# RWKV state chain of a hybrid decoder block: full 128x128 products in place of 32-column and 64-row ones

## Chip, cores and metric

One core of a Trainium2 chip runs the whole block. The metric is the device time of one execution in microseconds; three executions were timed, and one more was recorded by the hardware profiler.

## The reference, cut to what matters

The block takes 512 tokens of width 1024. It projects them, runs two groups of heads side by side (a sparse attention, "NSA", and a recurrent time mix, "RWKV-7"), joins both in an output projection, and ends with a gated feed-forward layer. The part that is changed is the recurrence, over 8 heads of 64:

```python
def _wkv7_step(state, inp):
    r, w, k, v, a, b = inp
    sa = jnp.einsum('bhvk,bhk->bhv', state, a)
    state = state * w[:, :, None, :] + sa[..., None] * b[:, :, None, :] + v[..., None] * k[:, :, None, :]
    return state, jnp.einsum('bhvk,bhk->bhv', state, r)
...
    _, y = lax.scan(_wkv7_step, state0, xs)
...
    mu = jnp.mean(y, axis=-1, keepdims=True)
    var = jnp.mean(jnp.square(y - mu), axis=-1, keepdims=True)
    y = ((y - mu) * lax.rsqrt(var + GN_EPS)).reshape(B, T, D_RWKV) * ln_w + ln_b
```

## The kernel before, in words

The recurrence is not run token by token. The 512 tokens are cut into 16 chunks of 32, and the 8 heads into four pairs `JJ[j]` of 128 rows; two pairs make a group `GG[g]` (g = 0, 1). `prep(j)` makes for each pair the decayed vectors: `AR` holds, by chunk c, 32 columns of a~ and 32 columns of r~ over the 128 rows of the two heads; `BKt` holds, by pair of chunks cp, 128 rows: for each of its two chunks 32 rows of b~ and 32 rows of k~; `UV` has the same rows, 32 of u (to be found) and 32 of v. `inverse(g)` solves the triangular system inside each chunk (a loop of 31 steps on DVE and POOL with a way through DRAM), and leaves `AR` with the solved a~ and `AV` with the part of u that does not depend on the state.

`chain(g)` then walks over the 16 chunks. `step(c)` does: product `pu` (tiles named rw<-Sb,AR: the 32 columns of a~ against the state `Sb`, for both pairs), a DVE addition of `AV` into `UV` (the u of this chunk), product `pd` (rw<-UV,BKt: the chunk's 64 rows of b~ and k~ against its 64 rows of u and v), and two DVE additions of `pd` to the decayed state `sw`, which give the next `Sb`. So `pu`, `UV`, `pd`, `Sb` follow each other 15 times, and all else has to fit around them. `y(py, cp)` makes the output of two chunks: products py<-UV,Mr (64 columns each) and, for each chunk, py<-Sb,AR (32 columns of r~ against the state), all summed in one PSUM tile `py`. `norm` normalizes four chunks (128 tokens), transposes them and multiplies by the gate.

A product's shape is written rows*columns of its stationary operand. In the whole program most are 128*128; `pu` and py<-Sb,AR are 128*32, `pd` is 64*128, py<-UV,Mr, rw<-UV,Ma and rw<-XT,At are 128*64. A product of f32 operands shows as two records in the trace, of f32r operands as one.

The order of the work is not that of the code. Every call on an engine is held by `_Order` and released in the order of `TURNS`, a packed list of numbers, and `SWAP` names those `tensor_tensor` calls that go to the other of DVE and POOL. So chain(0) runs beside the rest of `prep` and the input projection, and chain(1) beside the attention (`score`, `attend`: products mm<-K,Q, rp<-cct,L, ot<-ph,Vt, with ACT's casts `ph` and DVE's `pl` between). Every record carries line 210, the one that makes the held calls, so the profile is read by tile names.

Of the kernel before, what the change touches and what calls it, by code (L numbers as in the profile page):

```python
# [33 lines left out]
for _n, _w in (("ident", 128), ("mask", 128), ("reset", 512), ("sel", 2), ("ones", 1), ("row", 1)):  # L34
# [91 lines left out]
    "jDS=@xD7x)pvEUZZZEtKg}l2QgcWKerAzul2eLlq-5p2Y|;z8&>tgp2AQeT^)-G@(*`_->Jl?mC$kl!1Nk{n$CK{5!n~~m*m{3`OWSK>bkLVL1KVjm+EjC"
    "WSvzTC?a6XIc)z{Ap!Kz?XBMf!*%{6C@@pKxHf*(9ZAHw|**ZtR!ycsI^OBp4W+bgYTAhC!rscIXdDFaU9*5&e&rB>}zv`KOTGza2?&3aEY<@m@2#Js(oG"
    "XL%1>??Fut2)AZ=-P6{u^!0Ym{;>Ue%W7P3pTJ_1lA=J;M5bQU9v{rd%-^vNs*5nfsrSrmJ?<)TWDe;W@Q=RsW!j?W`fz;8{&T0;Y;0!U*UDOnT1^<TMc;"
    "7fm##*3y}r#C^NSIN-WRJg)t8B&CVLdGfT0H0N;Dli-;o6GV{G6lB>%Mjeg=Nl)MpZc=;sDQP}D@h2|u{<|E{e0V49C7(clj;>q5j7g#Y3=_lk<`|9vx}0"
    "lGgoqr2l_KUR#N(dalSF$3cjf<2IY~gI`GhNIDM^JTB%@gm$ERdDcHs*wB^y1TdA=bNFo%pL+sS0l2Od{C^y?ga;#r6+TnYAh;^^_0V>j06AI!yCz0Zb+F"  # L130
    "cDwrHMu6E@rAxZ+iqsYVx!K(LC&57*vXm`F%i=-gUrPu&heUNmyYGiF$FW!NjDt}^c${yj&azh6DZ|d7*A%Szbw$<a4k&11a)`%;!WvI`p}C`)q(KnBy~1"
    "20&j3Gb{4miy~S1REoqFtZdKzd)k6BnyLcCkShux(N$YVH`h!|rm3pIzG?9PmlXx4Wpb~}p@(1}fzqXYg$g7P|OUjTgD9wJqZc2)yF=s<@DK2S{2FWo39Z"
    "g45g;zBgBNihCq$s^-DTz&b4vq%&#U)XXJg*H*E>jd0NgaBdGN`CK&>Z7X-8gbEqIHx+Rb!J%Xf&$eSw^wt%$=kdjnT5^lkj-P=+pEkvr*U-^^`T)8P{fH"
    "be#s-k(@DON<Bm`Hzhn<GSK%vfka89)efPB=QM?p!{jgn=$oHnoVQX}(gQ>?-Yb9<dP7oZIzQj?Q1ch%qU6MH^r7)SuFj8NB!N+4GJdW|ieMaYkF8{5-Ft"
    "j`ZnQ=Yw%8JFa86!E6uKn+B<Cd#j<!hwW4aDWb$yiZt)BJ#2*)A$N)F2fALTk9{2km}UrtYX#e2a`y2o?aGgG$7*>F6X1BWU1tDLV-V7;u7b+TU8a+U9hw"
    "X&L5>tz-1&gN`bjWw7rOJx;paTzUgDpq;c>Jr-GaXrqbt<dEO?x`-;zR0NQ0yVQ)=VLxb$W6V)nD>25@^ft*J|t^2#0OZdAqGloX)7zV6+dU`NXFS`m<`O"
    "JRZn1@@g8TPbJa25^S#dd8=q+<sU+KVH`%M}?F{XN-RdmzH+9_53FN4@!8oqDM;N;t(H3Zd4xFinwWIbyJFSm@Fb>Nt6-=Cdst5Hy`nm4p(Td}=ljmu=g|"
# [1145 lines left out]
```

## Time and profile before

| what | value |
|---|---|
| three timed executions | 792.83, 798.37, 799.33 us, median 798.37 |
| profiled execution, its own time | 796.21 us |
| its span | 794.3 us |
| PE busy | 766.3 us, 96% of the span |
| DVE, ACT, POOL busy | 517.5, 359.6, 227.0 us |

The chains lie in the first 380 us: chain(0) from about 170 to 255, chain(1) from about 302 to 372. From there on the output projection and the feed-forward layer run, with PE busy nearly all the time. The span is the time between the first and the last record; the execution's own time is 1.9 us more.

### The profile page before, as it was taken

Reading aid. Unit: us, or ns where it says so; the run is one execution under the profiler, and the core shown is the slowest. Engines: PE = TensorE matmul, PEld = TensorE weight load, DVE = VectorE, ACT = ScalarE, POOL = GpSimd, SP = SyncE. Lnnn points to the kernel's source line nnn. Section 1 sums busy time; section 2 is a strip of 40 time slices with the busy share of each in tenths; the row PEclk is TensorE's granted clock in tenths of the full one; section 3 lists DMA queues with packets and bytes.
Section 4 is the critical chain, followed back from the end, with each engine's and each line's share of the span. In section 5 each row is a group of like instructions: output and inputs, shape, how many; then the busy total and the mean of one; then the engine's idle time right before and its main releaser. Section 6 shows DMA issues by size and latency. Waiting matters only on the chain.

```text
span 794.3 us, 12056 instructions
## 1 busy us (share of the span) xinstructions
PE 766.3 (96%) x4152; PEld 617.0 (78%) x4152; DVE 517.5 (65%) x1078; ACT 359.6 (45%) x779; POOL 227.0 (29%) x360
## 2 busy tenths in 40 slices
PE   8999999999799889999999999999999999999998
PEld 7878768887567678777788888888888888888886
DVE  5565786788878978887264876767766777143131
ACT  5435644465234766766452544444444445131120
POOL 3334353234767766786414000000000000000000
PEclk9999999999879999999999999999999999999999
DMA  6542214321123030002442223232222324153130
GB/s 211 168 157 88 83 51 85 82 59 34 26 49 57 14 67 2 14 15 94 145 133 80 94 92 104 82 106 90 97 87 99 105 83 126 46 172 129 44 119 27
DMA packets 59708, 67.87 MB, mean 85 GB/s; under 512 B 25710, under 2 KB 32686, under 8 KB 59648
## 3 DMA queue, kind: packets, MB, share of 16 engines
q1 hardware_dynamic: 59460, 67.10, 27.4%
q8 instruction: 33, 0.54, 0.3%
q14 instruction: 27, 0.22, 0.1%
q10 hardware_dynamic: 188, 0.02, 0.0%
HBM read 63.91 MB, written 3.18 MB: 84 GB/s over the span
## 4 chain that ended last, share of the span: by engine, by line
PE 86%; DVE 7%; POOL 3%; issue 2%; ACT 1%; DMA 1%; SPq 0%; DVEq 0%; POOLq 0%; ACTq 0%
PE mm L210 31%; PE rp L210 23%; PE rw L210 21%; PE ot L210 5%; PE pre L210 4%; PE py L210 2%; POOL Z L210 1%; DVE Z L210 1%; DVE sgw L210 1%; DMA raw<-in_wst 1%; DVE Sb L210 0%; DVE sw L210 0%; DVE Ma L210 0%; DVE UV L210 0%; DVE qd L210 0%
## 5 line engine op out<-in xcount | busy, mean ns | idle before, releaser
L210 ACT CAST hi<-raw 128x512 fp32r<-128x512 f32 (+3 forms) x212 | 117.4, 584 | 127.2 <-DMA raw<-in_fdn 67.2
L210 DVE TENSOR_TENSOR lo<-raw,hi 128x512 fp32r<-128x512 f32 (+3 forms) x179 | 118.3, 672 | 39.8 <-ACT hi L210 15.4
L210 DVE SCALAR_TENSOR_TENSOR uf<-zf,fvt,uf 128x512 f32<-128x512 f32 x88 | 65.7, 749 | 29.4 <-ACT uf L210 29.4
L210 ACT ACTIVATE uf<-zf,fvt 128x512 f32<-128x512 f32 x44 | 35.8, 816 | 98.4 <-DVE zf L210 98.4
L210 POOL MEMSET zf<- 128x2 f32 x44 | 4.2, 100 | 211.3 <-DVE uf L210 107.5
L210 POOL TENSOR_TENSOR lo<-raw,hi 128x512 fp32r<-128x512 f32 (+3 forms) x33 | 39.8, 1210 | 68.3 <-ACT hi L210 28.8
L210 PE MATMUL mm<-act,hi 128*128 128x512 f32 x176 | 55.2, 395 | 0.0
L210 PE MATMUL mm<-h2h,hi 128*128 128x512 f32 x128 | 50.7, 396 | 0.0
L210 PE MATMUL mm<-h2l,hi 128*128 128x512 f32 x128 | 50.5, 395 | 0.0
L210 PE MATMUL mm<-h2h,lo 128*128 128x512 f32 x128 | 50.5, 394 | 0.0
L210 PE MATMUL rw<-h2h,hi 128*128 128x512 f32 x112 | 44.3, 395 | 0.0
L210 PE MATMUL rp<-h2l,hi 128*128 128x512 f32 x112 | 44.2, 394 | 0.0
L210 PE MATMUL rw<-h2l,hi 128*128 128x512 f32 x112 | 44.2, 394 | 0.0
L210 PE MATMUL rp<-h2h,hi 128*128 128x512 f32 x112 | 44.1, 396 | 0.0
L210 PE MATMUL rp<-h2h,lo 128*128 128x512 f32 x112 | 44.1, 394 | 0.0
L210 PE MATMUL rw<-h2h,lo 128*128 128x512 f32 x112 | 44.1, 394 | 0.0
L210 POOL TENSOR_TENSOR L<-L,st 128x512 f32<-128x512 f32 (+1 forms) x41 | 38.9, 968 | 5.7 <-PE rw L210 2.3
L210 ACT ACTIVATE L<-L,st 128x384 f32<-128x384 f32 (+3 forms) x64 | 35.4, 557 | 8.2 <-DVE st L210 5.4
L210 PEld LDWEIGHTS mm<-act,hi 128*128 128x128 f32 x176 | 33.0, 188 | 7.8
L210 PE MATMUL mm<-K,Q 128*128 128x256 f32 (+3 forms) x128 | 34.0, 362 | 2.8 <-DVE pl L210 2.1
L210 PE MATMUL mm<-act,lo 128*128 128x512 f32 x88 | 34.7, 394 | 0.0
L210 PE MATMUL mm<-XH,hi 128*128 128x512 f32 x80 | 32.8, 412 | 0.7 <-ACT hi L210 0.7
(403 smaller groups left out, 1986.1 us busy)
## 6 DMA issues: line engine op xcount, KB each, us to landing
raw<-in_fup SPq DMA_DIRECT2D x88, 256.0 KB, 2.8
raw<-in_fdn SPq DMA_DIRECT2D x40, 256.0 KB, 3.3
raw<-in_wf SPq DMA_DIRECT2D x20, 256.0 KB, 3.0
xr<-in_xT SPq DMA_DIRECT2D x16, 256.0 KB, 3.0
raw<-in_wout SPq DMA_DIRECT2D x16, 256.0 KB, 2.8
raw<-in_wst SPq DMA_DIRECT2D x16, 192.0 KB, 3.3
w<-in_cw SPq DMA_DIRECT2D x8, 256.0 KB, 3.6
bias<-bvec SPq DMA_DIRECT2D x8, 256.0 KB, 3.4
```

The costliest lines, as they stand in the source:

```text
L210: self._o.held.append(lambda: f(*a, **k))
```

## The change

The diff, without the packed numbers of `TURNS` and `SWAP`, which are replaced as a whole:

```diff
@@ inverse(g)
-            S.copy(out=gr.AV[:, :, jj], in_=pg.rearrange("p (a x) -> p a x", a=4))
+            for c4 in range(4):
+                for half in range(2):
+                    S.copy(out=gr.UV[half][64 * (c4 % 2):64 * (c4 % 2) + 32, c4 // 2:c4 // 2 + 3:2, jj],
+                           in_=pg[32 * c4:32 * c4 + 32, half * 256:half * 256 + 256].rearrange("p (a x) -> p a x", a=2))
+
+        for jj, (o, z) in enumerate(((JJ[js[0]], gr.At.rearrange("p j a k -> p (j a k)")),
+                                     (JJ[js[1]], gr.AV.rearrange("p a j k -> p (a j k)")))):
+            o.BKz = (z.rearrange("p (c k) -> p c k", c=8), o.BKt)
+            S.copy(out=o.BKz[0][0:64], in_=o.BKt[0:64])
+            G.memset(o.BKz[0][64:128], 0.0)
+            G.memset(o.BKt[0:64], 0.0)
         G.memset(gr.Sb, 0.0)
@@ chain(g), step(c)
                 for jj in range(2):
-                    PE.matmul(pu[r4, jj * 128:(jj + 1) * 128], oo[jj].AR[:, c, 0, :], gr.Sb[:, cur, jj],
+                    PE.matmul(pu[:, jj * 128:(jj + 1) * 128],
+                              oo[jj].AR[:, 2 * cp:2 * cp + 2].rearrange("p c a t -> p (c a t)"), gr.Sb[:, cur, jj],
                               start=True, stop=True)
-                V.tensor_tensor(out=uv[ru], in0=pu[r4, 0:256].rearrange(w2, j=2), in1=gr.AV[r4, c // 4], op=ALU.add)
+                V.tensor_tensor(out=uv[ru], in0=pu[ru, 0:256].rearrange(w2, j=2), in1=uv[ru], op=ALU.add)
+            if c % 4 == 0:
+                gr.ys = t2("ys", "t2g")[:, 0:256]
+            if c:
+                S.copy(out=gr.ys[r4], in_=pu[64 * c2 + 32:64 * c2 + 64, 0:256])
             else:
-                V.tensor_copy(uv[ru], gr.AV[r4, 0])
+                V.memset(gr.ys[r4], 0.0)
...
-                PE.matmul(pd[:, jj * 128:(jj + 1) * 128], oo[jj].BKt[r2, cp], uv[r2, jj], start=True, stop=True)
+                PE.matmul(pd[:, jj * 128:(jj + 1) * 128], oo[jj].BKz[c2][:, cp], uv[:, jj], start=True, stop=True)
@@ y(py, cp)
-            for c in (2 * cp, 2 * cp + 1):
...
-                    PE.matmul(py[r4, jj * 128:(jj + 1) * 128], oo[jj].AR[:, c, 1, :], gr.Sb[:, c % 4, jj],
-                              start=False, stop=True, skip_group_check=True)
@@ norm(py, ys, tt)
+            V.tensor_tensor(out=yc, in0=py[:, 0:256], in1=ys, op=ALU.add)
```

One product `pu` now takes a~ and r~ of two chunks as its 128 columns. Of its 128 rows of result one quarter goes to `UV` (u) and one quarter is copied by ACT to `ys`, which `norm` adds to `py` on DVE; the other half is not used. So the 60 products py<-Sb,AR are gone. `pd` contracts all 128 rows: the rows of the other chunk meet zeros, in two copies of `BKt` (`BKz`): for even chunks one in the tiles of `At` and `AV` (which show as rw<-UV,At and rw<-UV,AV), for odd chunks `BKt` itself with its upper half cleared. The constant part of u is copied straight to its place in `UV` by 32 small copies in place of 4 large ones. `y` of two pairs of chunks is made together, ahead of their `norm`.

Over the whole of PE's order there are 3629 products before and 3569 now. Going through both orders with each product's shape, the shape of the array's tiles changes 196 times before and 110 times now: runs of 128*32 products 37 and none, of 64*128 products 45 and 19, of 128*64 products 29 and 34, and 3 runs of a 33*8 shape in both. DVE has 1080 instructions in both, ACT 686 and 748, POOL 365 and 381, SP 317 in both.

PE in chain(1), inside the attention; before, from one `pd` over a `pu` to the next `pd`:

```order
L210 MATMUL rw<-UV,BKt 128x128 x2
L210 MATMUL mm<-K_719,Q_662 128x512 x2
L210 MATMUL rp<-cct,L 128x128 x6
L210 MATMUL rw<-Sb,AR 32x128 x2
L210 MATMUL rp<-cct,L 128x128 x5
L210 MATMUL ot<-PcH,Vc 128x128
L210 MATMUL ot<-PcL,Vc 128x128
L210 MATMUL rw<-UV,BKt 128x128 x2
```

PE in the same chain now, from one `pu` over a `pd` to the next `pu`:

```order
L210 MATMUL rw<-Sb,AR 128x128 x2
L210 MATMUL rp<-cct,L 128x128
L210 MATMUL mm<-K_685,Q_666 128x512 x2
L210 MATMUL rp<-cct,L 128x128 x2
L210 MATMUL rw<-UV,BKt 128x128 x2
L210 MATMUL rp<-cct,L 128x128
L210 MATMUL py<-SG,g2t 128x128
L210 MATMUL rp<-cct,L 128x128
L210 MATMUL rw<-Sb,AR 128x128 x2
L210 MATMUL ot<-PcH,Vc 128x128
L210 MATMUL py<-UV,Mr 64x64 x8
```

The same kind of attention products stands between the chain's products, fewer of them from `pd` to the next `pu`, and the shape changes at the products of the chain are gone; those around py<-UV,Mr stay.

PE in chain(0), inside the input projection (ot, rp, mm with XH, XL are its products). Before:

```order
L210 MATMUL rw<-Sb,AR 32x128 x2
L210 MATMUL rp<-cct,rbk 128x128
L210 MATMUL ot<-hi,XL 128x320
L210 MATMUL ot<-hi,XH 128x320
L210 MATMUL ot<-lo,XH 128x320
L210 MATMUL ot<-hi,XL 128x320
L210 MATMUL rw<-UV,BKt 128x128 x2
```

PE in the same part of the program now:

```order
L210 MATMUL rw<-Sb,AR 128x128 x2
L210 MATMUL mm<-XH,hi 128x512
L210 MATMUL rw<-UV,At 128x128
L210 MATMUL rw<-UV,AV 128x128
L210 MATMUL ot<-hi,XH 128x320
L210 MATMUL rp<-rh,bones 128x512
```

From the third `pu` to its `pd` five products stood before; in this place of the new order one stands.

ACT at the end of inverse(1), where chain(1) begins. Before:

```order
L210 COPY AV<-rw 128x4x128
L210 CAST ph<-rp 128x512
L210 COPY of<-ot 64x256
L210 CAST ph<-rp 128x512 x2
L210 ACTIVATE L,st<-L,st 128x512
L210 COPY AR<-rw 128x16x32
L210 COPY AV<-rw 128x4x128
```

ACT at the same end of inverse(1) now:

```order
L210 COPY UV<-rw 32x2x128
L210 ACTIVATE L,st<-L,st 128x512
L210 COPY UV<-rw 32x2x128 x4
L210 COPY of<-ot 64x256
L210 COPY UV<-rw 32x2x128 x4
L210 COPY of<-ot 64x256
L210 COPY At<-BKt 64x1024
L210 COPY AV<-BKt 64x1024
L210 COPY UV<-rw 32x2x128 x2
L210 COPY AR<-rw 128x16x32 x2
L210 COPY UV<-rw 32x2x128 x3
```

The small copies to `UV` and the two copies of `BKt` stand close together, and the casts `ph` of the attention behind them.

PE at the same place, the new order only (before, no product of the chain's start depended on a copy of `BKt`):

```order
L210 MATMUL rw<-XT,At 64x128 x15
L210 MATMUL py<-SG,g2t 128x128
L210 MATMUL mm<-K_685,Q_706 128x256
L210 MATMUL rw<-UV,At 128x128
L210 MATMUL mm<-K_685,Q_666 128x128 x2
L210 MATMUL rp<-cct,L 128x128 x2
L210 MATMUL rw<-UV,AV 128x128
```

The first `pd` of chain(1) reads the copy of `BKt` that is written over `At`, and the last product that reads the old `At` stands two products ahead of it.

## Rows read from the trace of the kernel before

**Rows 1.** The page: span, and PE's busy time with its share and instructions

```profile
span 794.3 us, 12056 instructions
...
PE 766.3 (96%) x4152; PEld 617.0 (78%) x4152; DVE 517.5 (65%) x1078; ACT 359.6 (45%) x779; POOL 227.0 (29%) x360
```

**Rows 2.** Stretches: length, busy us of PE, PEld, DVE, ACT, POOL, granted clock, DMA

```profile
160.00:300.00 140.00, 124.44 (x927) 97.46 (x927) 116.09 (x306) 72.91 (x202) 88.03 (x139) 0.94 0.19 43
300.00:380.00 80.00, 78.07 (x580) 60.61 (x579) 66.11 (x195) 52.41 (x163) 55.18 (x82) 1.00 0.11 35
380.00:794.30 414.30, 409.95 (x1772) 330.75 (x1770) 227.99 (x350) 155.47 (x259) 24.30 (x60) 1.00 0.30 98
213.20:226.90 13.70, 12.64 (x69) 8.71 (x70) 9.96 (x20) 1.60 (x3) 7.53 (x12) 0.50 0.25 49
```

**Rows 3.** PE's groups by shape: count, busy us, mean ns, idle before

```profile
L210 PE MATMUL ot<-ph,Vt 128*128 128x512 f32 x40 | 17.5, 438 | 1.4 <-ACT ph L210 1.4
...
L210 PE MATMUL py<-Sb,AR 128*32 128x128 f32 x120 | 10.7, 299 | 0.0
```

**Rows 4.** Timeline of PE in chain(0): start us, length us, shape, records

```profile
230.72 0.27 PE L210 MATMUL rp<-cct,qd 128*128 128x128 f32 x1
230.92 0.62 PE L210 MATMUL rw<-Sb,AR 128*32 128x128 f32 x4
231.47 0.76 PE L210 MATMUL rp<-cct,qd 128*128 128x128 f32 x5
232.07 0.27 PE L210 MATMUL rp<-cct,kdup 128*128 128x128 f32 x1
232.28 0.71 PE L210 MATMUL rw<-UV,BKt 64*128 64x128 f32 x4
232.92 0.33 PE L210 MATMUL rp<-cct,kdup 128*128 128x128 f32 x1
```

**Rows 5.** Timeline of PE where py and rw products of 32 columns mix

```profile
239.28 0.30 PE L210 MATMUL rw<-Sb,AR 128*32 128x128 f32 x1
239.30 0.39 PE L210 MATMUL py<-Sb,AR 128*32 128x128 f32 x2
...
239.64 0.27 PE L210 MATMUL rw<-Sb,AR 128*32 128x128 f32 x1
```

**Rows 6.** Timeline of all engines, 210 to 214 us

```profile
210.42 2.73 DVE L210 TENSOR_TENSOR sw<-Sb,wcs 64x128 f32<-64x128 f32 x1
210.67 2.33 POOL L210 TENSOR_TENSOR qd<-qs,rq 128x256 f32<-128x256 f32 x4
...
213.62 0.61 PE L210 MATMUL rw<-Sb,AR 128*32 128x128 f32 x2 [3.88 <-DVE Sb L210]
```

**Rows 7.** Timeline of the shortest steps from pu to pd and from pd to pu

```profile
243.35 0.27 PE L210 MATMUL rw<-Sb,AR 128*32 128x128 f32 x1
...
244.21 0.71 PE L210 MATMUL rw<-UV,BKt 64*128 64x128 f32 x4
...
253.11 0.71 PE L210 MATMUL rw<-UV,BKt 64*128 64x128 f32 x4
...
254.71 0.52 PE L210 MATMUL rw<-Sb,AR 128*32 128x128 f32 x3
```

**Rows 8.** ACT's and POOL's groups: count, busy us, mean ns

```profile
L210 ACT CAST hi<-raw 128x320 fp32r<-128x320 f32 x8 | 3.7, 458 | 2.4 <-DMA raw<-in_wtB 0.7 <-PE rp L210 0.6 <-PE ot L210 0.5
L210 ACT COPY of<-ot 64x256 f32<-64x256 f32 x16 | 5.9, 367 | 4.5 <-PE ot L210 3.8 <-DVE of L210 0.5
L210 ACT COPY X<-kz 64x512 f32<-64x512 f32 x4 | 2.5, 620 | 8.8 <-DVE kz L210 8.8
L210 ACT COPY AR<-rw 128x512 f32<-128x512 f32 x4 | 2.2, 588 | 0.8 <-PE rw L210 0.8
L210 POOL MEMSET XT<- 128x1024 f32 x4 | 3.8, 955 | 0.0
```

**Rows 9.** DVE's groups from 160 to 382 us

```profile
L210 DVE TENSOR_TENSOR yb<-py,m 128x256 f32<-128x256 f32 x8 | 3.4, 425 | 0.3
```

More of the change, by code (lines that the diff above doesn't have):

```diff
@@ L170 @@
[L170 to L173 removed]
+    "c-rlnb-YzY_y0d@BW1wlN-IbzAPCYec<B(46e*DgA0(utyG0rWMZf|D44y|CDUs%q0tTJZ4YStwGy5D6gV*nm-@n}VYoB{|&8(SOvu1tvK2-sfPLNz;MeU"
@@ new lines @@
+    "y?l9EUuCGZH&nB)FUe%`bb_7EOIio3+Z_?IMs+T-w?N6G||Z^@7_qytHSbM_|A+j(AF1y%5DNHJ8v2@7~_Dq7-8J7k{nNRD#6f4A+ngJI3A0U7X<UA431S"
+    "jZE20)=@05xYRnkVGu=5j=`ZRsn+Y$cm?FYYA-N)eVrDb<`&ltpIk|AGSQG8d`LoZTf{YlSJ5W1FaEu+D_Ku&pgE=S4iaZilxPIdkkmoch>kD&)*_R5IL8"
+    "f7AM0k6D%^%4l)$+wCkW<w>X@%la`hJaL#~E34XWa@U6II7wxho!wt(u3$w93msrD@XnWMsBY%`eJa^KHp+tfU90|u7)8n?K!>_!fkR+j10TS~w36kJ~?X"
+    "tw&1Dqvf?;b(QkW?g=bzQM_Y=dVVxtee-Tl1S;X3s6L1H9vo{l1?(NrK~c+)jmDv0*5dU=ucBambM%IW7i=$U+>IqjHHHkpsbjU_Y-p$~%q(djjtz`{WaR"
@@ L645, in y, with norm @@
                 PE.matmul(py[64 * e:64 * e + 64, h * 64:(h + 1) * 64], oo[h // 2].Mr[:, h % 2, cp],
-                          gr.UV[cp // 4][:, cp % 4, h // 2, (h % 2) * 64:(h % 2) * 64 + 64], start=(h == 0), stop=False,
-                          skip_group_check=True)
-            for c in (2 * cp, 2 * cp + 1):
-                if c == 0:
-                    continue
-                r4 = slice(32 * (c % 4), 32 * (c % 4) + 32)
-                for jj in range(2):
-                    PE.matmul(py[r4, jj * 128:(jj + 1) * 128], oo[jj].AR[:, c, 1, :], gr.Sb[:, c % 4, jj],
-                              start=False, stop=True, skip_group_check=True)
-        def norm(py, tt):
-            yv = py[:, 0:256].rearrange(h4, h=4)
-            m8, v8 = sm("m8", 4, "smg"), sm("v8", 4, "smg")
-            V.tensor_reduce(out=m8, in_=yv, axis=AX.X, op=ALU.add)
-            V.tensor_scalar(out=m8, in0=m8, scalar1=-1.0 / 64, scalar2=None, op0=ALU.mult)
+                          gr.UV[cp // 4][:, cp % 4, h // 2, (h % 2) * 64:(h % 2) * 64 + 64], start=True, stop=True)
+        def norm(py, ys, tt):
             yb = t2("yb", "t2g")
             yc, sq = yb[:, 0:256], yb[:, 256:512]
+            V.tensor_tensor(out=yc, in0=py[:, 0:256], in1=ys, op=ALU.add)
             ycv = yc.rearrange(h4, h=4)
-            V.tensor_tensor(out=ycv, in0=yv, in1=bc(m8.rearrange("p (h o) -> p h o", o=1), [128, 4, 64]), op=ALU.add)
+            m8, v8 = sm("m8", 4, "smg"), sm("v8", 4, "smg")
+            V.tensor_reduce(out=m8, in_=ycv, axis=AX.X, op=ALU.add)
+            V.tensor_scalar(out=m8, in0=m8, scalar1=-1.0 / 64, scalar2=None, op0=ALU.mult)
+            V.tensor_tensor(out=ycv, in0=ycv, in1=bc(m8.rearrange("p (h o) -> p h o", o=1), [128, 4, 64]), op=ALU.add)
             for h in range(4):
@@ L689, in chain @@
             step(2 * cp + 1)
-            if cp % 2 == 0:
-                if cp:
-                    norm(py, cp // 2 - 1)
+            if cp % 2:
                 py = PS("py")
-            y(py, cp)
-        norm(py, 3)
+                y(py, cp - 1)
+                y(py, cp)
+                norm(py, gr.ys, cp // 2)
     Vc = const([128, 2, 4, 128], F32R, "Vc")
```

118 lines of the change are left out of this document (56 added, 62 removed).

## The prediction

> **What bounds the kernel now.** I read the page first: PE is busy 766.3 of 794.3 us [rows 1]. That share alone says little, since a record's length covers time in which the next product already runs, so I went on to the stretches [rows 2]. From 380 us on PE has hardly a gap (409.95 of 414.3 us), and nothing in that part is changed but the place of a few instructions; I leave it as it is. From 0 to 160 us no part of a chain runs, and the edits touch only the order there. The change must pay between 160 and 380 us. There PE is busy 202.5 of 220 us (124.44 + 78.07), DVE 182.2, ACT 125.3, POOL 143.2. So PE is the first limit of this stretch and DVE (83%) the next. PE's idle 17.5 us are mostly in the part up to 300 us (15.6), and the largest single one is 3.88 us before a `pu` at 213.62 [rows 6].
>
> **What a change of shape costs.** This is the main term. Two products of the same shape start 0.11 us apart: the five records at 231.47 take 0.76 us, of which the last is 0.27 long, so the four steps take 0.49 [rows 4]; the first and the last of four rw records of one kind lie 0.36 us apart, three steps [rows 5]. Where the shape changes, the distance grows. Into the 128*32 products: 230.72 to 230.92 is 0.20, that is 0.09 more, and the four records need 0.62 - 0.27 = 0.35 for three steps, 0.02 more. Out of them: the last starts at 231.27, the next shape at 231.47, 0.09 more, and the five steps there lose another 0.05. A visit costs 0.25 us, 0.13 for each change. Into and out of the 64*128 products it is more: 232.07 to 232.28 (0.10), 0.44 for three steps (0.11), 232.72 to 232.92 (0.09), and the same 0.05: 0.35 us, 0.18 for each [rows 4]. The new order has 110 changes where there were 196. I take 0.15 for each of the 86: **12.9 us**; the two ends give 11.2 and 15.5. All of it is PE time, and PE is what this stretch waits for; the part that falls where PE would have waited for DVE anyway is worth nothing, and 17.5 of 220 us is the measure of that, so the lower end for the term goes to 9 us.
>
> **The products removed.** 60 products py<-Sb,AR of two records each are gone [rows 3]. In a row by themselves, at 0.11, they would be 13.2 us. But they do not run by themselves: between 239.28 and 239.64 the four rw records keep the distance of a row by themselves, and six py records start among them, the first two at 239.28 and 239.30, into other columns of the array [rows 5]. There they cost nothing. Of the 18 runs in the old order that hold them, 12 hold rw products too; in the other six they alternate among two groups of columns, 0.055 us each. A third of 120 records at 0.055 is **2.2 us**; the ends are 0 and 6.6 (all at 0.055). The widened products cost no more than the narrow ones: 0.11 us from start to start holds for 128*128, 128*32 and 64*128 alike [rows 4, 5].
>
> Here a rule of the Trainium skill speaks against the change: the page "TensorE: Matmul & The Clock Gate", Part 3 (packing small matmuls), advises to give narrow products their own columns, since they then run at the same time, and measures 2.38 times for three of them. By it the 240 narrow records were worth 240 x 0.11 / 2.38 = 11.1 us, an estimate, and the 120 wide ones 13.2, a loss of 2.1 in place of my gain of 2.2, and the sum below would be 790, inside the range of the forecast itself. The trace agrees only where the narrow products stand together, which is in 12 of 37 runs.
>
> **What is added.** ACT gets 30 copies to `ys` and 32 to `UV`; the nearest row is of<-ot, 64x256, 0.367 us [rows 8]: 22.8 us. It loses 4 copies to `AV` at the 0.588 of AR<-rw, a copy of the same size: 2.4. The four copies of 64x1024 are each two of X<-kz, 1.24: 5.0. In sum 25.4 us on an engine that is idle for 94.7 of these 220 us [rows 2]; I cost it at nothing but for the chain's start, and ACT's idle time is the cover. POOL gets eight clears of 0.955 at most [rows 8], 7.6 us, in 77 idle us. DVE gets eight additions into `yc` at 0.425 [rows 9], 3.4 us, and gives eight calls to POOL by `SWAP`; its count does not change, and I take zero. SP issues as many transfers as before, and the DMA share in this stretch is 0.11 to 0.19 [rows 2]: nothing.
>
> **New waits, start of a chain.** The first `pd` of chain(1) reads the copy over `At`, which cannot begin before the last rw<-XT,At. That takes 0.27 for the product and 1.24 for the copy, and between the two the new order has a product of two records and one more, 0.33 us of PE work. PE waits 1.2 us. The second `pd` reads the copy over `AV`, ACT's next instruction: another 1.24 us, against 0.9 us of products: 0.4. Behind PE's wait stand the attention's products; behind ACT's copies its casts `ph`. In chain(0) the copy has an AR<-rw (0.588), a cast (0.458) and a small copy (0.367) ahead of it on ACT, 2.9 us with the product and itself, and PE has 1.8 us of projection in between: 1.2. Together **2.8 us** lost; zero if ACT runs ahead, and 6 if the clears on POOL (two of 0.955 behind another) come last.
>
> **New waits, steps set too close.** Last record of `pu` to the first of `pd` takes at least 0.86 us (243.35 to 244.21), and `pd` to `pu` 1.16 (253.55, the start of its fourth record, to 254.71) [rows 7]. Less the 0.11 of the record itself, 0.75 and 1.05 us of other work must stand between. I added up what stands there in the new order, record by record: in three places `pu` to `pd` has 0.23, 0.29 and 0.51, in three `pd` to `pu` has 0.66, 0.79 and 0.81. The missing time is 1.2 + 0.9 = **2.1 us**; before, only one place is below, by 0.01. All other places have 0.8 to 7 us.
>
> **The sum.** 12.9 + 2.2 - 2.8 - 2.1 = 10.2 us, from the profiled execution's 796.2: **786.0 us**. That execution lies 2.2 us below the median of the three (798.4), inside their spread of 6.5, and I make no correction. That spread is also why less than 1% cannot be told from no change here.
>
> **Rivals.**
> *Others take over.* DVE is at 83% and POOL feeds it; PE's faster pace would only wait for `L`, `pl` and `Sb`. For it: in 160 to 300 us PE already waits 15.6 us, with DVE busy 116 of 140. Against: from 300 to 380 PE waits 1.9 us with DVE at the same share, so that share alone does not stop PE. If half of the 15.1 us comes back as waits, it is 794; if all, 801.
> *ACT's copies reach the path (slower).* In the attention PE waits for ACT's `ph` before ot<-ph,Vt. The 25.4 us stand in a strict queue ahead of those casts. From 300 to 380 ACT is busy 52.4 of 80 us [rows 2]; with chain(1)'s share of the copies, 15 x 0.367 and half of the copies at its start, it comes to some 62 of 74. From the point at which 10.2 of the 25.4 us are exposed the change gains nothing; if 20 are, it is 806, and 811 if all are. For it: bunches of UV copies at the end of inverse(1). Against: ACT is idle a third of that stretch.
> *The big stall goes too (faster still).* The wait at 213.62 comes from one DVE multiplication `sw` that took 2.73 us beside POOL's `qd`, where the same shape otherwise takes some 0.3 [rows 6]. The granted clock was 0.50 (1.2 GHz) from 213.2 to 226.9 [rows 2], right behind it; up to half of these 13.7 us, 6.8, is lost there. An order in which the two do not meet gains up to 3.9 + 6.8 = 10.7 us more: 775. Nothing in an order tells whether two instructions meet in time; a new stall of the same kind at another place would cost as much.
> *The change of shape is not the cause.* If the 0.09 us at each change were waiting for operands and not the change itself, 86 fewer of them would save nothing: 799. Against it: the two gaps at 230.92 and 231.47 are alike to 0.01 us though one product waits for the chain and the other for nothing new.
>
> **How the numbers follow.** Chances: forecast, 776 to 792, 0.48; others take over, 791 to 801, 0.20; ACT, slower, 0.09; the big stall gone, 770 to 778, 0.16; not the cause, 0.07. From these: faster by over 1% (below 790.4) takes most of the first, the fourth and a quarter of the second, 0.68; within 1% 0.23; slower by over 1% 0.09. The range leaves out the far half of the fast case and the slow case: 773 to 799.
>
> **What would show it.** Right: PE's records of rw<-Sb,AR and rw<-UV with a 128*128 shape follow the attention's at 0.11 us, and the stretch that ends with chain(1) ends some 10 us sooner, with DVE's and ACT's shares higher. The chain's start should show a wait of PE of 1 to 2 us for ACT's copy. Wrong: PE's busy time falls by 15 us and its idle time rises by as much, with DVE or ACT as releaser; or ot<-ph,Vt waits for `ph` for far more than the 1.4 us of now [rows 3]; or the gain is in the first 160 us, which would mean that the new order did it and not the shapes.

## The result, and the profile after

The changed kernel is slower, by 1.3%. Its four runs took 807.01 to 808.85 us, median 807.58, beside 798.18 for the kernel before: a ratio of 1.0133 [1.0086, 1.0180]. Forecast were 786.0 us and a range from 773 to 799, so the measured time lies outside.

How times are compared below: the kernel before scatters from 786.3 to 801.1 us over the jobs (medians 791.97 to 798.18), while the runs of one version of the changed kernel lie within 0.7 to 6.8 us. So a version is read by its own median, by its ratio to the kernel before, and by how far its trace has shifted. Where the three differ, I give all.

The page of the changed kernel, to be held against [rows 1]:

```profile
span 807.0 us, 11911 instructions
...
PE 770.3 (95%) x4032; PEld 627.9 (78%) x4032; DVE 511.6 (63%) x1078; ACT 381.8 (47%) x841; POOL 235.9 (29%) x376
```

Its stretches (columns as in [rows 2]), the last one behind the wait that matters:

```profile
0.00:160.00 160.00, 153.53 (x855) 126.60 (x856) 96.51 (x199) 75.83 (x154) 64.79 (x92) 1.00 0.40 114
160.00:300.00 140.00, 123.13 (x821) 101.02 (x819) 110.71 (x309) 80.77 (x223) 88.12 (x142) 0.93 0.19 43
300.00:380.00 80.00, 73.47 (x538) 61.43 (x536) 67.48 (x204) 63.32 (x189) 55.22 (x79) 1.00 0.09 26
380.00:807.00 427.00, 420.20 (x1825) 338.86 (x1824) 236.93 (x369) 161.87 (x278) 27.79 (x64) 0.99 0.31 97
180.90:191.10 10.20, 9.29 (x47) 8.19 (x48) 1.38 (x2) 3.28 (x7) 1.89 (x2) 0.50 0.01 2
```

PE has 120 records fewer and yet 4 us more of busy time. From 160 to 300 us it does 821 records where it did 927, so work is pushed back, and the last stretch has 1825 records where it had 1772. The larger part of the loss arises ahead of 300 us. The first product `pd` of chain(0) (rw<-UV with `BKt` or its copy) comes at 194.03 us, and the last product `pu` of chain(1) at 378.73, which is 8.9 of the 12.7 us that the span is longer; the other 3.8 come behind it. Before, the two came here:

```profile
170.57 0.71 PE L210 MATMUL rw<-UV,BKt 64*128 64x128 f32 x4
...
369.83 0.30 PE L210 MATMUL rw<-Sb,AR 128*32 128x128 f32 x1
```

The timeline of PE in the changed kernel shows how chain(0) starts, and in its last two rows chain(1):

```profile
180.70 3.10 PE L210 MATMUL rw<-AV,XT 128*128 128x64 f32 x14 [1.89 <-ACT UV L210]
...
185.21 0.69 PE L210 MATMUL rw<-AV,XT 128*128 128x64 f32 x2 [0.45 <-ACT UV L210]
186.35 1.11 PE L210 MATMUL rw<-AV,XT 128*128 128x64 f32 x4 [0.45 <-ACT UV L210]
187.39 2.84 PE L210 MATMUL rw<-XT,At 128*64 128x128 f32 x18
...
194.03 0.39 PE L210 MATMUL rw<-UV,At 128*128 128x128 f32 x2
...
314.08 0.46 PE L210 MATMUL rw<-UV,At 128*128 128x128 f32 x2 [0.66 <-POOL At L210]
...
315.46 0.46 PE L210 MATMUL rw<-UV,AV 128*128 128x128 f32 x2 [0.50 <-ACT UV L210]
```

Products rw<-AV,XT wait for ACT's copies to `UV`, though no product reads what these copies write. They read columns 0 to 255 of the PSUM tile, and the products are still filling its columns behind 255. After the wait of 1.89 us the granted clock is 0.50 (1.2 GHz) for 10.2 us. ACT's timeline at the same place:

```profile
178.04 0.36 ACT L210 COPY UV<-rw 32x256 f32<-32x256 f32 x1 [2.17 <-PE rw L210]
178.64 0.62 ACT L210 CAST rh<-KR 128x512 fp32r<-128x512 f32 x1 [0.23 <-DVE KR L210]
179.16 0.22 ACT L210 ACTIVATE gt<-gt 128x24 f32<-128x24 f32 x1
179.29 0.60 ACT L210 CAST hi<-raw 128x512 fp32r<-128x512 f32 x1
179.91 0.74 ACT L210 COPY UV<-rw 32x256 f32<-32x256 f32 x2
```

The second and third copy stand behind three other instructions in ACT's queue, end at 180.65, and PE goes on at 180.70.

The chain also starts late because the first inverse ends late. Groups from 125 to 170 us on DVE and POOL, before:

```profile
L210 DVE TENSOR_TENSOR Z<-Z 128x30 f32<-128x30 f32 (+19 forms) x26 | 6.7, 259 | 2.2 <-POOL Z L210 1.0 <-POOL z L210 0.6
L210 DVE TENSOR_TENSOR Z<-Z,U 128x30 f32<-128x30 f32 (+18 forms) x26 | 6.6, 255 | 3.2 <-POOL Z L210 2.6
...
L210 POOL TENSOR_TENSOR Z<-Z,U 128x81 f32<-128x81 f32 (+4 forms) x5 | 2.1, 410 | 10.1 <-DVE Z L210 10.1
L210 POOL TENSOR_TENSOR Z<-Z 128x31 f32<-128x31 f32 (+4 forms) x5 | 2.0, 405 | 7.9 <-DVE Z L210 7.8
```

The same groups in the changed kernel:

```profile
L210 DVE TENSOR_TENSOR Z<-Z 128x126 f32<-128x126 f32 (+15 forms) x20 | 5.7, 283 | 7.6 <-POOL Z L210 6.1 <-POOL z L210 1.1
L210 DVE TENSOR_TENSOR Z<-Z,U 128x30 f32<-128x30 f32 (+15 forms) x19 | 4.8, 253 | 4.6 <-POOL Z L210 3.7 <-POOL z L210 0.5
...
L210 POOL TENSOR_TENSOR Z<-Z,U 128x120 f32<-128x120 f32 (+10 forms) x12 | 5.7, 476 | 12.3 <-DVE Z L210 6.6 <-DMA U<-Ld 4.4 <-DVE gt L210 0.8
L210 POOL TENSOR_TENSOR Z<-Z 128x110 f32<-128x110 f32 (+9 forms) x11 | 5.0, 452 | 3.7 <-DVE Z L210 3.4
```

Of the 62 instructions of this serial loop (31 steps of two) POOL had 10 and now has 23, at some 0.46 us each where DVE takes 0.27. The queue of SP, which issues the transfers, shows both ends of it in the changed kernel:

```profile
132.66 0.83 SPq L210 DMA_DIRECT2D raw<-in_wtA  x2
133.66 2.68 SPq L210 DMA_DIRECT2D U<-Ld  x4
...
166.18 1.29 SPq L210 DMA_DIRECT2D Zd<-Z  x2
```

And before:

```profile
124.34 3.61 SPq L210 DMA_DIRECT2D U<-Ld  x4
...
153.68 1.29 SPq L210 DMA_DIRECT2D Zd<-Z  x2
```

The loads that the loop starts from are issued 9.3 us later, behind weight loads for which SP waits 4.6 us for DVE, and the loop's result is stored 12.5 us later: the loop itself has grown by 3.2 us.

### The profile page after: what moved, and what is told of

It reads as the page before. It is cut to its first block, busy times and chain, and to the rows that moved or that the text cites. A ratio compares the mean times of both kernels' runs of the same rounds, so it can differ in the third digit from the quotient of the medians.

```text
span 807.0 us, 11911 instructions
## 1 busy us (share of the span) xinstructions
PE 770.3 (95%) x4032; PEld 627.9 (78%) x4032; DVE 511.6 (63%) x1078; ACT 381.8 (47%) x841; POOL 235.9 (29%) x376
## 4 chain that ended last, share of the span: by engine, by line
PE 75%; DVE 11%; POOL 5%; ACT 3%; issue 3%; DMA 3%; SPq 0%; DVEq 0%; POOLq 0%; ACTq 0%
PE mm L210 26%; PE rp L210 22%; PE rw L210 19%; PE pre L210 4%; PE ot L210 3%; POOL Z L210 3%; DVE Z L210 2%; PE py L210 1%; DVE pl L210 1%; DVE Sb L210 1%; POOL L L210 1%; DVE L L210 1%; DVE lo L210 1%; DMA fvt<-in_fv 1%; DMA U<-Ld 0%
## 5 line engine op out<-in xcount | busy, mean ns | idle before, releaser
L210 PE MATMUL rp<-h2l,hi 128*128 128x512 f32 x112 | 44.2, 395 | 0.0
L210 PE MATMUL rp<-h2h,lo 128*128 128x512 f32 x112 | 44.2, 394 | 0.0
L210 ACT ACTIVATE L<-L,st 128x128 f32<-128x128 f32 (+3 forms) x64 | 35.6, 559 | 0.8 <-DVE st L210 0.7
L210 PE MATMUL mm<-K,Q 128*128 128x384 f32 (+3 forms) x128 | 34.1, 352 | 0.6 <-DVE of L210 0.4
L210 PE MATMUL mm<-XH,lo 128*128 128x512 f32 x80 | 32.4, 404 | 1.0 <-DVE lo L210 0.9
```

The lines of the kernel that those rows point to most:

```text
L210: self._o.held.append(lambda: f(*a, **k))
```

## The experiments

Theories at first: A, the new order ahead of the chain costs the time, some 13 us in the first inverse and what leads to it, and the shapes gain as forecast; B, ACT's added copies cost it; C, the shapes gain little or nothing. All versions hold the changed code but for e4. Shift of the traces, in us:

| kernel | first chain product | last product `pu` | span | median | ratio to before |
|---|---|---|---|---|---|
| kernel before | 170.57 | 369.83 | 794.3 | 798.18 | 1 |
| changed kernel | 194.03 | 378.73 | 807.0 | 807.58 | 1.0133 |
| e5, inverse sooner | 189.56 | 373.94 | 800.6 | 802.95 | 1.0106 |
| e6, shapes back | 193.41 | 384.85 | 811.3 | 813.28 | 1.0241 |
| e7, no added copies | 187.11 | 367.56 | 792.8 | 793.22 | 0.9974 |
| e9, no r~ copies | 194.50 | 375.93 | 802.0 | 802.91 | 1.0160 |
| e13, no u copies | 184.52 | 367.66 | 795.8 | 798.21 | 1.0063 |
| e14, six copies moved | 187.00 | 372.04 | 800.3 | 799.81 | 1.0077 |
| e17, three repairs | 182.19 | 367.38 | 791.9 | 793.58 | 1.0012 |

A late start of the chain is not all lost: in e17 the first chain product still comes 11.6 us later than in the kernel before, and the two take the same time. The column serves to compare versions of the changed kernel with each other.

### Code and order taken apart: e1 to e4

```diff
 e1  code: changed   TURNS, SWAP: as before throughout
 e2  code: changed   as before up to the first chain product, new from there
 e3  code: changed   new up to the first chain product, as before from there
 e4  code: before    TURNS, SWAP: new throughout
```

> The changed kernel's code, issued in the order of the kernel before: each call that both kernels have keeps its place in that order (and its engine, DVE or POOL); the copies of r~'s rows stand right behind the addition of u, the copies of u's constant for the first eight chunks where the copy to AV stood, the others behind the chain's first two products, the zero-padding behind the last product that reads its buffer, and 36 of 6014 calls wait up to 49 places for a buffer. Theory A (the new order costs, the new products save): the changed kernel lost some 13 us ahead of the chain's first product and 4 us after 437 us by its order; without it 788 to 797 us, at least 10 below the changed kernel. Rival B (the added copies, clears and waits cost, in any order): 804 or more. Rival C (fewer changes of shape give nothing, the order takes something): 798 as before.

> The changed kernel's code; all that stands ahead of the first chain's first product in the order of before is issued in that order, all the rest in the new order. Theory A: the 13 us that are lost ahead of the chain come back, the 4 us at the second norm's wait may not: 792 to 798 us, and the chain's first product starts near 171 us instead of 194. Rival B: 804 to 808 us, since the copies and the chain are as in the changed kernel. Rival C: between, 800.

> The reverse: the changed kernel's code, in the new order until the first chain's first product, and from there in the order of before. Theory A: the loss ahead of the chain stays, so 802 to 810 us, and the chain's first product near 194 us. Rival B: 804 to 810 too, so this run tells apart only whether the new order is worth something inside the chain: by A some 3 us worse than the changed kernel, by C the same.

> The code of before (32-row products, y's r~ products) in the new order; y's products of every even pair of chunks stand behind the second product of the step after it, since the state's buffers turn over, and ten calls wait up to 16 places for a buffer. Theory A: 808 to 820 us, since the order ahead of the chain loses its 13 us with the old code too, and the chain pays for its changes of shape. Rival B: 797 to 803, since none of the added work is there. Rival C: 807, the order alone.

Measured: e1 830.68 (1.0497 [1.0414, 1.0579]), e2 796.66 (1.0022 [0.9984, 1.0059]), e3 843.62 (1.0647 [1.0579, 1.0715]), e4 816.18 (1.0295 [1.0228, 1.0363]). Crossing code and order (e1, e3, e4) costs 20 us and more over the kernel before: an order fits the code that it was made for. Theory A had e4 right (808 to 820) and missed e1 (788 to 797) and e3 (802 to 810) by far. A group of PE in e1, 160 to 420 us, shows a part of it:

```profile
L208 PE MATMUL rw<-UV,At 128*128 128x128 f32 x32 | 7.7, 322 | 7.7 <-DVE UV L208 3.3 <-ACT UV L208 2.7 <-ACT ys L208 1.3
```

There the chain's products meet copies that the old order has no place for. This is 7.7 of the 29 us by which PE is busy less from 160 to 400 us (192.78 us in place of 221.84); what else e1 loses, and what e3 and e4 lose, was not taken apart. So these crossings can't be added up. But e2 says one thing: with the old order ahead of the chain, 11 us are back by the medians and 8.9 by the ratios, and no gain appears. Its first chain product comes at 183.09, not near 171 as theory A had it.

### The first inverse alone: e5

```diff
-SP: raw<-in_wtA x2; U<-Ld x4               inverse(0): 23 of 62 instructions on POOL
+SP: raw<-in_wtA; U<-Ld x4; raw<-in_wtA     inverse(0): 10 of 62 instructions on POOL
```

> The changed kernel with two touches to its order alone, both ahead of the first chain. The substitution of the first inverse runs on the engines that it had before (10 of its 62 operations on POOL instead of 23), and the four loads of U are issued ahead of two weight loads that made SP wait 4.6 us. Theory A (the order delays the first inverse, and TensorE runs out of other work while it waits): the substitution ends 6 to 9 us sooner than at 166.1 us and the kernel takes 3 to 9 us less than the changed one, a ratio to before of 1.002 to 1.010. Rival B (the added copies, clears and waits are the loss): the inverse ends sooner, the total stays within 2 us of the changed kernel, ratio 1.011 to 1.016.

802.95 us (801.32 to 804.98), 1.0106 [1.0067, 1.0145]. One of the two weight loads, not both, has gone behind the loads of `U`. These are issued at 130.59 in place of 133.66, and the store `Zd` at 161.67 in place of 166.18: by the trace 3.1 us come from the loads and 1.4 from the engines of the loop, and no run has one without the other. Theory A had expected 6 to 9 us. The first chain product comes 4.5 us sooner; the time falls by 4.6 by the medians, 6.4 by the spans and 2.2 by the ratios. The trace after it is the old one, moved, with PE's wait at the chain's start as it was:

```profile
176.23 3.25 PE L209 MATMUL rw<-AV,XT 128*128 128x64 f32 x14 [1.90 <-ACT UV L209]
```

Of theory A's 13 us the inverse thus holds a third by the medians, and a sixth by the ratios.

### The shapes alone: e6

```diff
-PE.matmul(pu[:, ...], oo[jj].AR[:, 2 * cp:2 * cp + 2].rearrange("p c a t -> p (c a t)"), ...)
+PE.matmul(pu[r2, ...], oo[jj].AR[:, c].rearrange("p a t -> p (a t)"), ...)
-PE.matmul(pd[:, ...], oo[jj].BKz[c2][:, cp], uv[:, jj], ...)
+PE.matmul(pd[:, ...], oo[jj].BKz[c2][r2, cp], uv[r2, jj], ...)
```

> The changed kernel, with the same calls in the same order; only the shapes of the chain's products go back to the narrow forms: the product for u takes one chunk's 64 columns a~|r~ (128*64) instead of two chunks' 128, and the product for the state reads the 64 rows that are not zero (64*128). The results are the same. By the forecast's price of a change of shape (0.15 us, some 110 to 120 changes more) it takes 8 to 17 us longer than the changed kernel, ratio to before 1.024 to 1.035. Rival C (the gaps lie beside waits that are there anyway): within 2 us of the changed kernel, ratio 1.011 to 1.016.

813.28 us (812.74 to 815.63), 1.0241 [1.0203, 1.0278]: 5.7 us more by the medians, 6.7 from the first chain product to the last in the trace, 8.6 by the ratios. The order has 220 changes of shape in place of 110, so one change costs 0.05 to 0.08 us, and not 0.15. From the first chain product to the last, in the changed kernel:

```profile
194.03:378.73 184.70, 166.05 (x1179) 135.98 (x1178) 159.19 (x473) 124.92 (x371) 133.00 (x206) 0.97 0.15 37
```

And in e6:

```profile
193.41:384.85 191.44, 177.58 (x1179) 135.65 (x1178) 160.37 (x473) 124.89 (x370) 132.29 (x206) 0.96 0.15 36
```

With the same 1179 records PE is busy 11.5 us less in the changed kernel, some 0.10 us for each change (a little of it is the clock, 0.97 against 0.96), but idle 18.65 us in place of 13.86. So 4.8 of the 11.5 us come back as waits, and 6.7 are left. The groups of `pu` and `pd`, 160 to 400 us, in e6:

```profile
L210 PE MATMUL rw<-Sb,AR 128*64 128x128 f32 x120 | 21.3, 297 | 1.5 <-DVE Sb L210 1.4
...
L210 PE MATMUL rw<-UV,BKt 64*128 64x128 f32 x56 | 10.8, 309 | 1.7 <-DVE UV L210 1.2 <-ACT ksw L210 0.4
```

And in the changed kernel:

```profile
L210 PE MATMUL rw<-Sb,AR 128*128 128x128 f32 x120 | 21.1, 294 | 3.0 <-DVE Sb L210 2.8
...
L210 PE MATMUL rw<-UV,BKt 128*128 128x128 f32 x56 | 10.5, 307 | 2.5 <-DVE UV L210 2.0 <-ACT ksw L210 0.4
```

With the full shape PE is idle 2.3 us longer before these products, nearly all of it for DVE's `Sb` and `UV`: here one sees part of what the shapes save turn into waits of the chain.

### The added copies: e7, e9, e13

```diff
-S.copy(out=gr.UV[half][...], in_=pg[...])      # e7, e13: the 32 copies of u's constant left out
-S.copy(out=gr.ys[r4], in_=pu[...])             # e7, e9: the 30 copies of r~'s rows left out
```

Without r~'s copies `norm` adds a tile of zeros, and without u's copies u starts from what its buffer held: these three versions do less than the block needs.

> The changed kernel without the copies that the change gave to ACT in the chain and in the inverse's tail: the 30 copies of the r~ rows (y then adds a tile of zeros) and the 32 copies of u's constant (u then starts from what the buffer held) are left out, so y and the state are not the reference's; the zero-padding stays. Theory A: 3 to 6 us less than the changed kernel (the waits for these copies at the two chain starts, 3.3 us in the trace), ratio 1.005 to 1.010. Rival B: 10 us or more less, ratio below 1.001.

> The changed kernel without the 30 copies of the r~ rows alone (y adds a tile of zeros instead, so y is not the reference's); the 32 copies of u's constant stay. The run without both kinds took about 14 us less than the changed kernel. If the copies of u's constant at the two chain starts are the cost (theory A2: TensorE waits for the PSUM banks that they hold, and the clock falls behind that), this run stays within 4 us of the changed kernel: ratio to before 1.008 to 1.014. If the r~ copies load ACT all along the chains (rival B2), it takes 8 us or more less: ratio 1.003 or below.

> The changed kernel without the 32 copies of u's constant alone (u starts from what its buffer held, so the results are not the reference's); the 30 copies of the r~ rows stay. Theory A2 (the waits and the clock at the first chain's start are the larger part): 796 to 800 us, some 8 to 11 less than the changed kernel, its first product for the state near 187 us instead of 194. Rival B2 (ACT's time along the chains): 802 to 805 us.

e7: 793.22 us (790.79 to 794.76), 0.9974 [0.9952, 0.9997]. e9: 802.91, 1.0160 [1.0122, 1.0198]. e13: 798.21, 1.0063 [1.0028, 1.0097]. With all copies out the time falls by 14.4 us by the medians, 14.2 by the spans and 12.7 by the ratios, so theory B has the place right. By the medians of e13 9.4 of them hang on u's copies (11.2 by the spans, 5.6 by the ratios), by e9 4.7 on r~'s; in the trace of e9 the last `pu` comes 2.8 us sooner, and the ratio of e9 shows no gain at all, so that r~'s copies are worth between nothing and 5 us. Even without any of the 62 copies the time is only 0.26% below that of the kernel before.

### The place of six copies: e14

```diff
 each of the two PSUM tiles of inverse(0)'s rw<-AV,XT:
 PE   products into columns 0 to 255
-ACT  three of the four copies UV<-rw of columns 0 to 255
 PE   products into columns 256 to 511
+ACT  the same three copies
```

> The changed kernel with one touch to its order: the six copies of u's constant that are issued between the products of the bank that they read (three in each bank of the first inverse) stand behind that bank's last product; nothing is left out. Theory A2: TensorE no longer waits 1.9, 0.45 and 0.45 us there, and the 10.2 us at half clock that begin there go or shrink: 3 to 7 us less than the changed kernel, 800 to 804 us, the first product for the state at 188 to 191 us. Rival B2: ACT's time is the same, so 806 to 809 us.

799.81 us (797.23 to 802.16), 1.0077 [1.0046, 1.0109]. No instruction was taken away, and 7.8 us are gone by the medians, 6.7 by the spans, 4.5 by the ratios. PE's timeline in e14:

```profile
178.79 1.67 PE L209 MATMUL rw<-AV,XT 128*128 128x64 f32 x14
...
180.64 1.00 PE L209 MATMUL rw<-AV,XT 128*128 128x64 f32 x8
181.57 1.54 PE L209 MATMUL rw<-XT,At 128*64 128x128 f32 x18
...
187.00 0.46 PE L209 MATMUL rw<-UV,At 128*128 128x128 f32 x2
```

The window of this stretch in e14:

```profile
176.00:195.00 19.00, 18.04 (x142) 15.96 (x140) 11.41 (x28) 14.43 (x37) 11.56 (x13) 1.00 0.10 26
```

And in the changed kernel:

```profile
176.00:195.00 19.00, 16.20 (x101) 14.66 (x100) 6.55 (x10) 9.02 (x20) 7.21 (x8) 0.73 0.10 22
```

The same products stand without a wait, the clock stays at 1.00 (2.4 GHz), and eighteen rw<-XT,At take 1.54 us where they took 2.84. All that follows is 7.0 us sooner. The three waits are 2.8 us together. The other 4.2 go with the clock: the changed kernel does the rest of this stretch at 0.50 for 10.2 us, e14 at 1.00. That e13, which has none of these copies, gains little more (1.6 us by the medians of the same job) says that their place costs the time and not ACT's work on them.

### Half of the copies on DVE: e10, e12, e16

```diff
-S.copy(out=gr.UV[half][...], in_=pg[32 * c4:32 * c4 + 32, ...])
+(S.copy if c4 < 2 else _vcopy)(out=gr.UV[half][...], in_=pg[32 * c4:32 * c4 + 32, ...])  # e10, e12
+(_vcopy if c4 % 2 else S.copy)(out=gr.UV[half][...], in_=pg[32 * c4:32 * c4 + 32, ...])  # e16
```

`_vcopy` calls `V.tensor_copy`. e10 is the changed kernel with this alone; e12 and e16 start in the old order and have the later place of the products py<-cct,rstdB, as e8 below.

> The changed kernel in its own order, with 16 of the 32 copies of u's constant on DVE instead of ACT, at the same places in the order. Theory A2: the two chain starts wait less for ACT (3.3 us in the trace), and with that one of the stretches at half clock (10.2 us) may go: 2 to 6 us less than the changed kernel, ratio 1.006 to 1.011. Rival B2: within 2 us, ratio 1.011 to 1.016.

> The kernel of the former mixture with three repairs (order of before until the first inverse's end, then the new one; ratio 1.003), in which TensorE waited 2.8 us for a cast that stood on ACT behind the copies of u's constant, and DVE 9.3 us. Here half of those copies are on DVE, and the cast and the activation that DVE waited for stand ahead of them. Theory A2: the wait and the 10.2 us at half clock behind it go, 785 to 792 us, ratio 0.987 to 0.996. Rival B2: 793 to 797, ratio 0.998 to 1.004.

> The order of before until the first inverse's end, then the new one, with the copies of u's constant split by row groups between ACT and DVE, and behind the cast and the subtraction for which TensorE waited 2.8 and 3.8 us in the two former versions; the second normalisation's tail 12 products later. Theory A2: no wait over 1.5 us is left between 160 and 190 us, 785 to 791 us, under the 792 to 798 that the kernel before takes on these chips. Rival B2: 793 to 797.

Misses, all three: 809.67 (1.0248 [1.0206, 1.0291]), 794.71 (1.0033 [1.0002, 1.0064]) and 795.61 (1.0021 [0.9988, 1.0054]). Two engines don't copy faster than one. ACT's timeline in e16:

```profile
168.26 0.36 ACT L208 COPY UV<-rw 32x256 f32<-32x256 f32 x1 [0.48 <-DVE UV L208]
169.11 0.36 ACT L208 COPY UV<-rw 32x256 f32<-32x256 f32 x1 [0.48 <-DVE UV L208]
```

DVE's there:

```profile
167.81 0.42 DVE L208 COPY UV<-rw 32x256 f32<-32x256 f32 x1 [1.09 <-ACT UV L208]
168.66 0.42 DVE L208 COPY UV<-rw 32x256 f32<-32x256 f32 x1 [0.43 <-ACT UV L208]
```

They take turns: a pair needs 0.85 us, and ACT alone, in e14, makes eight in 2.77 us, 0.35 each. What they share is the PSUM tile that they read. By the order of the calls in e16, ACT's copy at 168.26 writes the other of the two tiles `UV` than DVE's copy at 167.81, for which it waits. By that of e10, two copies write one tile `UV` out of two PSUM tiles, and they run at the same time. ACT's timeline there, and DVE's, where it is the first of the two:

```profile
193.39 0.36 ACT L210 COPY UV<-rw 32x256 f32<-32x256 f32 x1
```

```profile
193.39 0.88 DVE L210 COPY UV<-rw 32x256 f32<-32x256 f32 x2
```

### Repairs put together: e8, e11, e15, e17, e18

```diff
 e8   old order up to the first inverse's end, copies spread on ACT, new order then
 e11  changed kernel + e5 + half of the copies on DVE (e10)
 e15  changed kernel + e5 + e14 + copies split by c4 % 2 (as e16)
 e17  changed kernel + e5 + e14, all copies on ACT
 e18  old order up to inverse(0)'s products, new order then, with e14
 all five: products py<-cct,rstdB, of the normalization ahead of the feed-forward layer, twelve products later
```

> The changed kernel's code in the order of before until the end of the first inverse, with the added copies spread between other ACT work there, then the new order, and at the second normalisation all that follows the sum of squares 12 TensorE products later. Against the earlier mixture of orders (ratio 1.002) this takes away a wait of 4.7 us for the copies of u's constant and one of 2.6 us at the second normalisation, and two stretches at half clock behind them (6.8 and 3.4 us). Theory A: 783 to 791 us, ratio 0.985 to 0.995. Rival B: what the copies cost shows in another place, ratio 0.998 to 1.004.

> The changed kernel in the new order with three repairs together: the first inverse on its former engines with its loads ahead of the two weight loads (alone: 4.6 us less), half of the copies of u's constant on DVE, and all that follows the second normalisation's sum of squares 12 TensorE products later (a wait of 2.6 us and 3.4 us at half clock). Theory A2: 794 to 800 us, ratio 0.998 to 1.005, if the three add up; rival B2: only the first and the last count, 800 to 803, ratio 1.005 to 1.010.

> The new order with four repairs: the first inverse on its former engines and its loads first (4.6 us alone), the copies of u's constant behind their banks, half of them on DVE by their row groups (rows 64 to 95 on DVE, 0 to 31 on ACT, so that no two of a pair write interleaved columns of the same rows, as those did that took turns before), and the second normalisation's tail 12 TensorE products later. Theory A2: 793 to 799 us. Rival B2: 800 to 804.

> The new order with three repairs and all copies on ACT: the six copies behind their banks (799.8 us alone), the first inverse on its former engines with its loads first, and the second normalisation's tail 12 products later. If the repairs add up (theory A2): 790 to 795 us, ratio 0.992 to 1.000. If the first chain's start has other work that takes their place (rival D): 796 to 800, ratio 1.001 to 1.006.

> The order of before until the first product that uses the first inverse, from there the new order with the six copies behind their banks, and the second normalisation's tail 12 products later. Theory A2: 786 to 792 us, ratio 0.988 to 0.997, since the front of before has lost 5 us less by 160 us and the chain's start of the repaired order loses 8.7 us from 160 to 200 us against 12 to 15 in the former mixtures. Rival D: 793 to 797, ratio 0.998 to 1.003.

e8 795.14 (1.0034 [0.9999, 1.0070]), e11 804.59 (1.0189 [1.0150, 1.0227]), e15 797.79 (1.0054 [1.0016, 1.0092]), e17 **793.58** (1.0012 [0.9986, 1.0038]), e18 795.29 (1.0027 [1.0001, 1.0053]). e17 takes 14.0 us off the changed kernel by the medians: e5's 4.6 and e14's 7.8 add up to 12.4, and the place of the products py<-cct,rstdB has what is left, 1.6. By the ratios it is 9.7, with 2.2, 4.5 and 3.0. By the traces it is 15.1: the chain starts 4.5 us sooner in e5 and 7.0 in e14, and the time from the last `pu` to the end falls from 428.3 in the changed kernel to 424.5 in e17. That last part begins here in the changed kernel:

```profile
437.91 1.05 PE L210 MATMUL py<-cct,rstdB 128*128 128x1 f32 x8 [2.21 <-DVE rstdB L210]
```

In e17 the same products stand at 427.17 without a wait. But versions without this repair also differ in that last part, from 425.2 us (e7) to 428.3.

The changed code, repaired, is as fast as the kernel before. No version that does all the work beat it. e8, e12, e16 and e18 were expected to, by theory A or its successors, and e11 to come down to 800: these five missed. e11, with the split copies, is slower than e5 alone. e17 is in its range by the time (790 to 795), and by the ratio in that of its rival (1.001 to 1.006). No run has e17 without r~'s copies, so whether the shapes' gain would show then stays open.

## Why the prediction was wrong, point by point

**"From 0 to 160 us no part of a chain runs, and the edits touch only the order there."** The first step that failed. The stretch holds the serial loop that the chain waits for, and the forecast put what happens there at nothing. The new order moved 13 of the loop's instructions to POOL and its loads behind weight loads. Shown by e5: 4.6 us (4.5 in the trace, 2.2 by the ratios). The issue order had both, and I read it only around the chains. Of the 12.5 us by which the loop ends late, 9.3 are its late loads and 3.2 its own length; e5 mends 4.5, and the rest I did not take apart.

**New waits at the start of chain(0), priced at 1.2 us.** The price counted what the first `pd` reads, the copy over `At`. It missed copies that stand between products of one PSUM tile. Shown by e14: 7.0 us in the trace (7.8 by the medians, 4.5 by the ratios), of which the waits are 2.8 and the rest goes with the clock. For chain(1) I had 1.2 and 0.4; the trace has 0.66 and 0.50, the first for POOL's clearing of `At`.

The trace shows PE's products waiting for copies of other columns of the same tile, and copies on two engines taking turns on it. The Trainium skill, page "PSUM — Partial Sum Buffer", section "PSUM bank collisions raise a hardware error", says that accesses of different engines are to be kept apart by bank and by group of 32 partitions, whatever the addresses, two readers included. The trace agrees as to columns (the wait of 1.89 us) and as to two readers (the 0.48 us before each copy). In e16 the two engines read different groups of 32 partitions and still took turns, so this program waits more widely than the rule asks: by the whole PSUM tile, as e16 and e10 show, and not by the tile `UV` that the copies write. Read against the order, this rule would have named the six copies.

**0.15 us for a change of shape, 12.9 us in sum.** The mechanism is right, the size is not. Shown by e6: 0.05 to 0.08 us, so that 86 changes are worth 4.5 to 6.7 us. I took the price from starts in a stretch without waits and carried it to all places. In e6 a change costs PE some 0.10 us of busy time, and of this four tenths are lost again (4.8 of 11.5 us), because where the chain waits for DVE, time saved on PE is only waited for. I had lowered the end of the term to 9 for that, and it was not enough.

**The 60 products removed, 2.2 us, and the rule on packing** that spoke for a loss of 2.1 (Trainium skill, "TensorE: Matmul & The Clock Gate", Part 3): open. e6 has narrower forms, but not the separate products, and no run separates the two.

**25.4 us on ACT at nothing.** For the attention this holds: `ot<-ph,Vt` waited 1.4 us for `ph` [rows 3] and now never does. r~'s copies cost up to 4.7 us (e9), not settled more closely. The rival "ACT's copies reach the path" named 806 to 811 at 0.09, and the time fell there. But its mechanism, casts of the attention queued behind 25 us of copies, did not occur: it is the place of the copies. That its number fits is luck.

**Steps too close, 2.1 us; the rival of DVE taking over.** PE's waits for `Sb` and `UV` ahead of `pu` and `pd` add up to 6.9 us (2.8 and 4.1) where they had 7.0 (4.0 and 3.0), and products py<-UV,Mr now wait 1.6 us for `UV`. Whether the 2.1 us came as priced can't be told from these sums. The one of 3.88 us at 213.62 [rows 6] is gone, and shorter ones have come. So the third rival's stall went, but the time at half clock did not: from 225 to 235 us the granted clock is 0.51. Why it falls there, behind no wait above 0.55 us, stays open.

**"From 380 us on ... I leave it as it is."** Products py<-cct,rstdB wait 2.21 us for DVE, and 3.4 us at a clock of 0.50 follow at 440.3. In e17 the wait is gone, and the clock is 1.00 from 425 to 445 us. What this is worth is less sure: 1.6 us by e17's remainder in the medians, 3.0 in the ratios, up to 3.8 in the traces, and no run has it alone.

Put together: the forecast's -10.2, and on it 8.4 for the shapes (12.9 less 4.5), 3.7 for r~'s copies (between 2.8 and 4.7), 6 for the six copies beyond the 1.2 priced, 4.5 for the inverse, and 1.6 for py<-cct,rstdB, make +14. With the ratios throughout (6.2, nothing, 3.3, 2.2 and 3.0) they make +4.5. Measured is +10.6 by the ratio, 6.9 to 14.4 by its interval, between the two, so the terms give the sign and the rough size and no more. With its repairs e17 should stand at +1.9, the forecast's -10.2 with the 8.4 and the 3.7 on it; measured is +1.0.

## What to carry to other kernels

When a change comes with a new issue order, read the order of everything that the changed part waits for, not only of that part: count on which engine each step of a serial loop sits, and look for reads of a PSUM tile between products into it. In this program such reads belonged behind the tile's last product, and splitting them over two engines gained nothing, since they took turns. A price per event that is read where nothing waits is an upper bound for places where the chain waits anyway.

## What was not expected of the hardware

- A wait of PE of 1.89 us was followed by 10.2 us at a granted clock of 0.50 (1.2 GHz), in which PE was busy 9.29 us; without the wait (e14) the clock stayed at 1.00. From 150 to 400 us the changed kernel has 20.4 us at half clock, the kernel before 17.0, e14 and e17 10.2, e7 6.8, e1 37.4 and e3 44.2; but e8 has 20.4 as well, at 795.14 us, so the clock alone doesn't rank the versions.
- Two engines that copy from one PSUM tile take turns in this program and need 0.85 us for two copies, one engine alone 0.70.
- In the kernels before and after, an instruction of the small serial loop takes 0.25 to 0.28 us on DVE and 0.41 to 0.48 on POOL, and DVE's idle time behind POOL's steps rose from 3.6 to 9.8 us when POOL had 23 of them in place of 10.
